# Swapping high and low weight products in every second column block of a two-layer trunk

## The chip, the cores and the metric

The kernel runs on one core of a Trainium2 chip. The metric is the device time of one launch in microseconds. The kernel before took 800.97 us (median of three runs, 798.78 to 801.15). All rows below are from one profiled execution, which took 801.64 us; its instructions span 799.9 us.

## The reference

Two pre-norm residual layers on 256 tokens of width 1024, in float32. Cut to what matters:

```
h = x
for i in range(2):
    hn = rmsnorm(h, norm_mix[i])
    h = h + (short_conv_mixer(hn) if i == 0 else dilated_attention_mixer(hn))
    h = h + square(relu(rmsnorm(h, norm_mlp[i]) @ mlp_w_up[i])) @ mlp_w_down[i]
    h = h + sigmoid(rmsnorm(h, norm_ple[i]) @ ple_w_gate[i]) * (p[i] @ ple_w_proj[i])
return rmsnorm(h, norm_final)
```

Layer 0's mixer is a gated short convolution (`h @ w_in` split into B, C and X, then `w_out`). Layer 1's is attention with 8 heads in 3 groups, with rotary on part of each head. Nearly all of the arithmetic is the product of 256 token rows with large weight matrices: about 140 MB of weights are read once.

## The kernel before

**Split products.** A float32 product is built from products of rounded parts. Each weight slab arrives by DMA as `raw` (128 partitions by up to 1024 columns, 512 KB). ScalarE (ACT) rounds it to `whi` (L332, in `split_to`), and VectorE (DVE) makes the rest `wlo = raw - whi` (L281, in `sub`). Activations are split the same way into a pair tile, high part and low part side by side. A product then needs high by high, high by low and low by high.

**Three kinds of block.** `block` (L364 issues every weight matmul) has three forms, named by the plan. Kind "n" issues three matmuls of 256 columns into one half of an accumulator. Kind "t" swaps the operands, with 384 or 512 columns. Kind "w", the one that the change touches, issues two: a short one of 256 columns (`wlo` against the high activations) and a long one of 512 columns (`whi` against high and low activations side by side), into an accumulator (one PSUM bank) of its own. Each matmul has its own 128 by 128 weight load, shown as PEld.

**The plan.** `make_plan` writes out by hand the order of all blocks. In kind "w" two neighbouring column blocks, half 0 and half 1, always follow each other for the same row block `k`, each into its own bank: half 0, half 1, next `k`, half 0, half 1. Kind "w" is used in the X part of the convolution's input (accumulators `acc_X`), in both MLPs' up products (`acc_u`), in three quarters of the down products (`acc_d`; the last quarter is kind "n"), and in the query and key products of heads 1 to 7 (`acc_qk`). Behind the last row block stands a step that adds the two halves of each accumulator, one copy on ACT (L383) and one add on DVE (L384) for half 0 and then for half 1.

**The order on the engines.** TensorE (PE) takes the blocks in the plan's order. For ACT, DVE and GpSimd (POOL) a scheduler decides, from modelled times, how the steps' instructions and the weight splits are interleaved. Each engine takes its own queue in order. There are five `raw` and six split buffers, so splits run up to five slabs ahead of PE.

**Attention's side work.** For each head and group the added sums go to POOL, which applies the rotary (L607, L610, L616, the step `qk_out`). For group 0 the result is split again on ACT (L403) and DVE (L281, `qk<-qk,qk`). The step `scores` (PE L639, L642) writes two banks, DVE takes the masked maximum (L645, L648), ACT the exponential (L649) and the scaling (L651), and the step `turn` transposes the result on PE (L660, `tp`).

Of the kernel before, what the change touches and what calls it, by code (L numbers as in the profile page):

```python
# [205 lines left out]
def width(key):  # L206
    return {"v": GROUPS, "gate1": 4, "proj1": 4}.get(key, 1)
# [32 lines left out]
def tile_trunk(ctx: ExitStack, tc: tile.TileContext, plan, slabs, ap, out):  # L240
# [25 lines left out]
    def bank(name):  # L266
        return psum.tile([P, 2, S], F32, tag="ps", name=name)
# [9 lines left out]
    def flat(t):  # L277
        return t.rearrange("p i s -> p (i s)")
# [57 lines left out]
    def weights(item):  # L336
        si, at = place[item]
        split_to(si + min(LOOK, 1 + si // 3))
        hi, lo = parts[si]
        n = width(item[0]) * P  # L340
        return hi[:, at : at + n], lo[:, at : at + n]

    def block(kind, key, k, col, name, half, operand, m=0, cuts=1):
        name = (*name, half) if kind == "w" else name
        if name not in opened:
            acc[name] = bank("acc_" + "_".join(map(str, name)))
        left[name, half if kind == "n" else 0] -= 1
        whi, wlo = weights((key, k, col))
        x = state[operand][k // 2]
        if kind == "n":  # L350
            dst = acc[name][:, half, :]
            products = ((dst, wlo, x[0][:, k % 2, :]), (dst, whi, x[1][:, k % 2, :]), (dst, whi, x[0][:, k % 2, :]))
        elif kind == "w":

            dst = acc[name]
            products = ((dst[:, 0, :], wlo, x[0][:, k % 2, :]), (flat(dst), whi, flat(x[2][:, k % 2, :, :])))
        else:
            n = width(key) * P // cuts
            whi, wlo = (t[:, m * n : (m + 1) * n] for t in (whi, wlo))
            dst = flat(acc[name])[:, :n]  # L360
            xhi, xlo = (t[:, k % 2, half * P : (half + 1) * P] for t in x[:2])
            products = ((dst, xhi, whi), (dst, xhi, wlo), (dst, xlo, whi))
        for n, (to, a, b) in enumerate(products):
            nc.tensor.matmul(  # L364
                to,
                a,
                b,
                start=n == 0 and name not in opened,
                stop=n == len(products) - 1 and left[name, half if kind == "n" else 0] == 0,
                skip_group_check=True,  # L370
            )
            opened.add(name)
# [394 lines left out]
    for op in plan:  # L767
        if op[0] != "do":
            block(*op)
        elif op[1] in URGENT:  # L770
            with tc.high_priority(offset=HURRY):
                steps[op[1]](*op[2:])
        else:
            steps[op[1]](*op[2:])
# [87 lines left out]
```

## Time and profile before

| What | us |
|---|---|
| Median of three runs | 800.97 |
| Profiled execution | 801.64 |
| Span of its instructions | 799.9 |
| PE busy | 780.3 (98%) |
| DVE busy | 583.1 (73%) |
| ACT busy | 442.6 (55%) |
| POOL busy | 179.0 (22%) |

The profile's page lists busy time by engine, the granted TensorE clock in 40 slices, the chain that ended last, and groups of instructions by source line. A matmul's end is modelled, so the duration of one says less than the distance between the starts of two. In the groups, `lo` and `hi` in a tile's name are the low and high part of the weights.

### The profile page before, as it was taken

How to read it: one execution, taken by the hardware profiler on the slowest of the kernel's cores; microseconds unless marked ns; L12 is line 12 of the kernel's file. 1: busy time of each engine (PE TensorE's matmuls, PEld its weight loads, DVE VectorE, ACT ScalarE, POOL GpSimd, SP SyncE). 2: the span in 40 equal slices, each digit the busy share in tenths (PEclk: the TensorE clock that was granted, in tenths of full speed). 3: DMA queues.
4: the chain of work that ended last, by engine and by line, in shares of the span. 5: the costliest groups of instructions: out<-in, count | busy, mean ns of one | idle time of the engine just before them, and what ended most of it. 6: DMA issues, size and time to landing. Idle time of an engine off the chain costs nothing.

```text
span 799.9 us, 12768 instructions
## 1 busy us (share of the span) xinstructions
PE 780.3 (98%) x4986; PEld 713.9 (89%) x4986; DVE 583.1 (73%) x818; ACT 442.6 (55%) x672; POOL 179.0 (22%) x117
## 2 busy tenths in 40 slices
PE   8999999999999999995999999999999999999996
PEld 8999998888888999985999999999988888888985
DVE  6987778898456669747688779778598777555555
ACT  7655565666444447526647546656475655444453
POOL 0000000000000000397487678668000000000001
PEclk9999999999999999998999999999999999999998
DMA  8865565555555555643464455447556656556521
GB/s 280 298 213 192 182 187 176 193 180 189 184 184 186 185 165 170 197 125 103 161 185 157 150 168 169 158 148 213 172 155 185 196 183 188 183 185 186 184 79 54
DMA packets 41676, 140.98 MB, mean 176 GB/s; under 512 B 4752, under 2 KB 5136, under 8 KB 41616
## 3 DMA queue, kind: packets, MB, share of 16 engines
q1 hardware_dynamic: 41616, 140.17, 55.3%
q8 instruction: 39, 0.64, 0.3%
q14 instruction: 21, 0.17, 0.1%
HBM read 139.10 MB, written 1.05 MB: 175 GB/s over the span
## 4 chain that ended last, share of the span: by engine, by line
PE 89%; POOL 3%; DVE 3%; ACT 1%; issue 1%; DMA 1%; SPq 0%; POOLq 0%; DVEq 0%; ACTq 0%
PE acc_d L364 23%; PE acc_u L364 23%; PE acc_qk L364 13%; PE acc_v L364 7%; PE acc_o L364 6%; PE acc_g L364 5%; PE acc_B L364 3%; PE acc_X L364 3%; PE acc_C L364 3%; POOL rot L610 2%; DVE wlo L281 1%; PE tp L660 1%; PE o L681 1%; PE sc L642 1%; POOL qk L616 1%
## 5 line engine op out<-in xcount | busy, mean ns | idle before, releaser
L281 DVE TENSOR_TENSOR wlo<-raw,whi 128x1024 fp32r<-128x1024 f32 (+3 forms) x273 | 366.8, 1353 | 130.2 <-ACT whi L332 129.2
L332 ACT ACTIVATE whi<-raw 128x1024 fp32r<-128x1024 f32 (+3 forms) x273 | 276.4, 1017 | 191.3 <-PE acc_d L364 88.3
L364 PE MATMUL acc_d<-u,whi 128*128 128x512 f32 (+1 forms) x640 | 181.8, 352 | 0.0
L364 PE MATMUL acc_u<-x,whi 128*128 128x512 f32 x512 | 181.0, 399 | 0.0
L364 PE MATMUL acc_d<-u,wlo 128*128 128x256 f32 x512 | 144.1, 281 | 0.0
L364 PE MATMUL acc_u<-x,wlo 128*128 128x256 f32 x512 | 143.7, 281 | 0.0
L364 PE MATMUL acc_qk<-x,whi 128*128 128x512 f32 (+1 forms) x432 | 134.5, 368 | 0.0
L364 PEld LDWEIGHTS acc_d<-u,whi 128*128 128x128 f32 x640 | 112.1, 190 | 18.1
L436 POOL TENSOR_TENSOR n<-v,power 128x4 f32<-128x4 f32 (+1 forms) x6 | 6.5, 1085 | 516.7 <-DVE v L456 514.0
L364 PEld LDWEIGHTS acc_u<-x,whi 128*128 128x128 f32 x512 | 96.1, 188 | 23.8
L364 PE MATMUL acc_qk<-x,wlo 128*128 128x256 f32 x384 | 107.8, 281 | 0.0
L364 PEld LDWEIGHTS acc_d<-u,wlo 128*128 128x128 f32 x512 | 97.1, 190 | 0.0
L364 PEld LDWEIGHTS acc_u<-x,wlo 128*128 128x128 f32 x512 | 96.7, 189 | 0.0
L364 PEld LDWEIGHTS acc_qk<-x,whi 128*128 128x128 f32 x432 | 77.8, 188 | 13.6
L610 POOL TENSOR_TENSOR rot<-qk,sinr 16x512 f32<-16x512 f32 x48 | 88.2, 1838 | 3.3
L364 PEld LDWEIGHTS acc_qk<-x,wlo 128*128 128x128 f32 x384 | 72.4, 189 | 0.0
L364 PE MATMUL acc_v<-whi,x 128*128 128x384 f32 x256 | 69.4, 342 | 0.0
L607 POOL TENSOR_TENSOR qk<-qk,cosr 128x512 f32<-128x512 f32 x24 | 37.6, 1565 | 56.2 <-DVE qk L384 39.5
L364 PEld LDWEIGHTS acc_v<-whi,x 128*128 128x128 f32 x256 | 47.0, 190 | 0.0
L364 PE MATMUL acc_o<-y,whi 128*128 128x256 f32 x256 | 46.0, 283 | 0.0
L616 POOL TENSOR_TENSOR qk<-qk,rot 48x512 f32<-48x512 f32 x24 | 43.7, 1822 | 1.7
L364 PE MATMUL acc_v<-wlo,x 128*128 128x384 f32 x128 | 43.1, 337 | 0.0
(164 smaller groups left out, 1036.4 us busy)
## 6 DMA issues: line engine op xcount, KB each, us to landing
raw<-in_w SPq DMA_DIRECT2D x232, 512.0 KB, 3.6
raw<-in_w SPq DMA_DIRECT2D x32, 384.0 KB, 3.1
raw<-in_w SPq DMA_DIRECT2D x7, 256.0 KB, 5.3
h<-in_xT SPq DMA_DIRECT2D x4, 256.0 KB, 5.6
out<-ht SPq DMA_DIRECT2D x4, 256.0 KB, 2.0
pt<-in_pT SPq DMA_DIRECT2D x2, 256.0 KB, 4.4
mask<-in_mask SPq DMA_DIRECT2D x2, 256.0 KB, 4.2
gain<-in_gain SPq DMA_DIRECT2D x2, 256.0 KB, 4.3
```

What stands on the lines that cost most here:

```text
L281: nc.vector.tensor_tensor(out, a, f32(b), ALU.subtract)
L332: nc.scalar.activation(hi[:, :width], t[:, :width], AF.Copy)
L364: nc.tensor.matmul(to, a, b, start=n == 0 and name not in opened, stop=n == len(products) - 1 and left[name, half if kind == "n" else 0] == 0,
L436: nc.gpsimd.tensor_tensor(y, v, power[:, : v.shape[1]], ALU.pow)
L607: nc.gpsimd.tensor_tensor(t, p, both(cosr), ALU.mult)
L610: nc.gpsimd.tensor_tensor(r[dst : dst + 16], p[src : src + 16], sinr[src : src + 16].unsqueeze(1).to_broadcast([16, 2, S]), ALU.mult,)
L616: nc.gpsimd.tensor_tensor(t[:48], t[:48], r[:48], ALU.add)
L642: nc.tensor.matmul(ps[:, (g + 1) * P : (g + 2) * P], t[:, 0, own], t[:, 1, own], start=True, stop=True)
L660: nc.tensor.transpose(ps[n // 2][:, n % 2, b * P : (b + 1) * P], sm[:, n * P : (n + 1) * P], ident)
L681: nc.tensor.matmul(ps[:, 0, b * P : (b + 1) * P], v12[:, b, g * P : (g + 1) * P], t[:, g, b * P : (b + 1) * P], start=False, stop=g == 1, ...
```

## The change

Where the block is the second of two neighbours (`half` is 1) and of kind "w", its two matmuls change places: the long one with `whi` comes first and the short one with `wlo` behind it. The first of the two keeps its order. Two lines stand more in the source, so every line below them has a number that is higher by two (L364 becomes L366).

```
@@ -354,6 +354,8 @@
 
             dst = acc[name]
             products = ((dst[:, 0, :], wlo, x[0][:, k % 2, :]), (flat(dst), whi, flat(x[2][:, k % 2, :, :])))
+
+            products = products[::-1] if half else products
         else:
```

On PE, in the X part of the convolution, before (the digit behind `acc_X_0` is the half; 128x256 is the short one):

```order
67 L364 MATMUL acc_X_0_0_335<-x0_0_139,whi9_274 128x512
68 L364 MATMUL acc_X_0_1_350<-x0_0_139,wlo9_275 128x256
69 L364 MATMUL acc_X_0_1_350<-x0_0_139,whi9_274 128x512
70 L364 MATMUL acc_X_0_0_335<-x0_0_139,wlo9_275 128x256
71 L364 MATMUL acc_X_0_0_335<-x0_0_139,whi9_274 128x512
```

The same place after the change:

```order
67 L366 MATMUL acc_X_0_0_335<-x0_0_139,whi9_274 128x512
68 L366 MATMUL acc_X_0_1_350<-x0_0_139,whi9_274 128x512
69 L366 MATMUL acc_X_0_1_350<-x0_0_139,wlo9_275 128x256
70 L366 MATMUL acc_X_0_0_335<-x0_0_139,wlo9_275 128x256
71 L366 MATMUL acc_X_0_0_335<-x0_0_139,whi9_274 128x512
```

Short, long, short, long has become short, long, long, short. This happens at 648 pairs of blocks; PE's order is otherwise the same, except that at the first `acc_u` of layer 1 before had short, short, long, long.

The scheduler answers on ACT and DVE. On ACT, where the sums of head 4, group 0 are made, before:

```order
344 L332 ACTIVATE whi157_4727<-raw157_4625 128x768
345 L383 ACTIVATE qk_4_0_4747<-acc_qk_4_0_0_4701 128x256
346 L383 ACTIVATE qk_4_0_4747<-acc_qk_4_0_1_4710 128x256
347 L332 ACTIVATE whi158_4792<-raw158_4643 128x768
348 L649 ACTIVATE sm3_0_4765,st2_3_0_4768<-sm3_0_4765,st1_3_0_4767 128x512
```

The same place after the change:

```order
344 L332 ACTIVATE whi157_4727<-raw157_4625 128x768
345 L385 ACTIVATE qk_4_0_4747<-acc_qk_4_0_0_4701 128x256
346 L332 ACTIVATE whi158_4792<-raw158_4643 128x768
347 L385 ACTIVATE qk_4_0_4747<-acc_qk_4_0_1_4710 128x256
348 L651 ACTIVATE sm3_0_4765,st2_3_0_4768<-sm3_0_4765,st1_3_0_4767 128x512
```

A weight split now stands between the copies of half 0 and half 1. The same happens at nearly every sum of two halves, on ACT and on DVE (there `wlo158` moves in front of the add of half 1).

On DVE, where the scores of head 0 are taken (`sc0`, with the sums of head 1 around them), before:

```order
358 L384 TENSOR_TENSOR qk_1_2_3964<-acc_qk_1_2_0_3888,qk_1_2_3964 128x256
359 L384 TENSOR_TENSOR qk_1_2_3964<-acc_qk_1_2_1_3897,qk_1_2_3964 128x256
360 L645 ISA sm0_0_3940,st0_0_0_3941<-sc0_0_3934,mask0_3461 128x512
361 L645 ISA st0_0_0_3941 128x1
362 L281 TENSOR_TENSOR wlo132_3977<-raw132_3834,whi132_3976 128x1024
363 L648 TENSOR_SCALAR st1_0_0_3942<-st0_0_0_3941 128x1
364 L645 ISA sm0_1_3955,st0_0_1_3956<-sc0_1_3949,mask1_3463 128x512
365 L645 ISA st0_0_1_3956 128x1
366 L648 TENSOR_SCALAR st1_0_1_3957<-st0_0_1_3956 128x1
```

The same place after the change:

```order
358 L386 TENSOR_TENSOR qk_1_2_3964<-acc_qk_1_2_0_3888,qk_1_2_3964 128x256
359 L647 ISA sm0_0_3940,st0_0_0_3941<-sc0_0_3934,mask0_3461 128x512
360 L647 ISA st0_0_0_3941 128x1
361 L386 TENSOR_TENSOR qk_1_2_3964<-acc_qk_1_2_1_3897,qk_1_2_3964 128x256
362 L650 TENSOR_SCALAR st1_0_0_3942<-st0_0_0_3941 128x1
363 L647 ISA sm0_1_3955,st0_0_1_3956<-sc0_1_3949,mask1_3463 128x512
364 L647 ISA st0_0_1_3956 128x1
365 L281 TENSOR_TENSOR wlo132_3977<-raw132_3834,whi132_3976 128x1024
366 L650 TENSOR_SCALAR st1_0_1_3957<-st0_0_1_3956 128x1
```

The split `wlo132` has moved from behind the first maximum to behind the second; the same nine instructions stand in front of and including `st1_0_1`. POOL's and SP's orders are unchanged.

## Rows read from the trace of the kernel before

**Rows 1.** The page: busy us (share) and instructions; the chain by engine.

```profile
PE 780.3 (98%) x4986; PEld 713.9 (89%) x4986; DVE 583.1 (73%) x818; ACT 442.6 (55%) x672; POOL 179.0 (22%) x117
PE 89%; POOL 3%; DVE 3%; ACT 1%; issue 1%; DMA 1%; SPq 0%; POOLq 0%; DVEq 0%; ACTq 0%
```

**Rows 2.** PE's waits: engine, line, waited for; us in total, times, longest.

```profile
PE tp L660 <- ACT sm L651: 8.7, 1, 8.7
```

**Rows 3.** The chain in order of time: start us, us, engine, tile, line, matmuls.

```profile
48.96 5.76 PE acc_C L364 x48
54.72 5.64 PE acc_X L364 x32
...
530.76 11.11 PE acc_qk L364 x64
...
603.62 67.84 PE acc_u L364 x384
671.46 90.87 PE acc_d L364 x576
762.33 5.47 PE acc_g L364 x24
```

**Rows 4.** Groups by line and shape: how many long matmuls of kind "w".

```profile
L364 PE MATMUL acc_u<-x,whi 128*128 128x512 f32 x512 | 181.0, 399 | 0.0
L364 PE MATMUL acc_d<-u,whi 128*128 128x512 f32 x384 | 135.8, 399 | 0.0
L364 PE MATMUL acc_qk<-x,whi 128*128 128x512 f32 x336 | 117.2, 392 | 0.0
L364 PE MATMUL acc_X<-x,whi 128*128 128x512 f32 x64 | 22.8, 398 | 0.0
```

**Rows 5.** Timeline of PE and PEld in an up product: start us, us.

```profile
160.45 0.28 PE L364 MATMUL acc_u<-x,wlo 128*128 128x256 f32 x1
160.45 0.19 PEld L364 LDWEIGHTS acc_u<-x,whi 128*128 128x128 f32 x1
...
160.57 0.40 PE L364 MATMUL acc_u<-x,whi 128*128 128x512 f32 x1
...
160.81 0.28 PE L364 MATMUL acc_u<-x,wlo 128*128 128x256 f32 x1
```

**Rows 6.** Timeline of PE at the first `acc_u` of layer 1.

```profile
580.54 0.40 PE L364 MATMUL acc_u<-x,wlo 128*128 128x256 f32 x2
580.78 0.70 PE L364 MATMUL acc_u<-x,whi 128*128 128x512 f32 x2
581.31 0.28 PE L364 MATMUL acc_u<-x,wlo 128*128 128x256 f32 x1
```

**Rows 7.** Timeline of PEld there.

```profile
580.74 0.30 PEld L364 LDWEIGHTS acc_u<-x,whi 128*128 128x128 f32 x2
```

**Rows 8.** Timeline of DVE, then ACT, around the scores of head 0.

```profile
367.24 2.32 DVE L281 TENSOR_TENSOR wlo<-raw,whi 128x1024 fp32r<-128x1024 f32 x1
...
370.26 0.15 DVE L648 TENSOR_SCALAR st<-st 128x1 f32<-128x1 f32 x1
...
370.45 0.72 ACT L649 ACTIVATE sm<-sm,st 128x512 f32<-128x512 f32 x1
```

**Rows 9.** Timeline of ACT, DVE and POOL in head 4; then PE's chain.

```profile
442.21 0.84 ACT L332 ACTIVATE whi<-raw 128x768 fp32r<-128x768 f32 x1
...
451.43 0.71 ACT L651 ACTIVATE sm<-sm,st 128x512 f32<-128x512 f32 x1
...
440.09 1.71 DVE L281 TENSOR_TENSOR wlo<-raw,whi 128x768 fp32r<-128x768 f32 x1 [0.26 <-ACT whi L332]
...
453.44 6.40 DVE L281 TENSOR_TENSOR wlo<-raw,whi 128x768 fp32r<-128x768 f32 x3 [0.25 <-ACT whi L332]
...
442.85 1.28 POOL L607 TENSOR_TENSOR qk<-qk,cosr 128x512 f32<-128x512 f32 x1 [1.87 <-DVE qk L384]
...
454.61 0.87 PE tp L660 x8
```

More of the change, by code (lines that the diff above doesn't have):

```diff
@@ L356, in block @@
             products = ((dst[:, 0, :], wlo, x[0][:, k % 2, :]), (flat(dst), whi, flat(x[2][:, k % 2, :, :])))
+            products = products[::-1] if half else products
         else:
```

## The prediction

> **What bounds the kernel now.** The page comes first. PE is busy for 780.3 us of the span of 799.9, and the chain that ended last is PE for 89% of it [rows 1]. So the end moves only if PE's own work gets shorter or longer, or if PE waits at a place where it doesn't now. PE's waits come second: the one of any size is 8.7 us, once, where the transposes of head 0 wait for ACT's scaled scores [rows 2]. The chain in order of time comes third, because it gives the price of a matmul by division, which the single durations don't (their ends are modelled and overlap).
>
> From the chain [rows 3], short and short: 5.76 us / 48 = 120 ns for a 256-column matmul behind its like. Long and long: 5.47 / 24 = 228 ns for a 512-column one behind its like. So a matmul costs (228 - 120) / 256 = 0.42 ns a column and some 12 ns on top, and a pair of short and long should cost 348 ns. The query and key pairs of the heads cost just that: 11.11 / 32 = 347 ns. The other pairs of the same form do not: X 5.64 / 16 = 352.5 ns, up 67.84 / 192 = 353.3 ns, and down, with its last quarter of 192 short matmuls taken off, (90.87 - 192 x 0.120) / 192 = 353.3 ns. These pairs pay 6.3 ns more than a head's pair does, and the reader is to see that no column, load or wait in the rows accounts for it.
>
> The timeline of an up product says where it is paid [rows 5]: the short one starts at 160.45, the long at 160.57, the next short at 160.81. Short to long is 0.12 us, as among equals; long to short is 0.24 where 0.228 would do. The weight load of the next matmul starts when the present one starts and takes 0.19, so loads run beside the matmuls in this order too.
>
> **The change, part by part.**
>
> *PE's order.* No matmul, load, column or wait is added or removed. Two pairs, short-long-short-long, become short-long-long-short. Per two pairs there were two steps from short to long and two from long to short; now there is one of each, one long-long and one short-short. Affected are the long matmuls of kind "w": 64 in X, 512 up, 384 down, together 960 that pay 6.3 ns, and 336 in the heads that pay nothing extra [rows 4].
>
> What the new steps cost: long-long 228 and short-short 120, from the rows above. What becomes of the 6.3 ns, no row of a whole stage shows, since there the order alternates always. The bounds: if each step from long to short goes on paying its extra, half of those steps remain and 960 x 6.3 / 2 = 3.0 us go. If the extra belongs to strict alternation, all of it goes, 6.1 us. If it belongs to a short and a long together, whatever their order, nothing goes.
>
> One place of before holds the new order by accident, the first up product of layer 1 [rows 6]: two short from 580.54, two long from 580.78, the next short at 581.31. These four take 0.77 us, but the first of the two high loads starts at 580.74 [rows 7], where it would have started with the second short at 580.66, that is 0.08 late. Without that the four take 0.69 us, against 2 x 353.3 = 707 ns for two pairs of up and 694 for two of the heads. Read to 0.01 us, it is nearer to the price without the extra, but it is one place right behind a stall. I take the middle between half and all, 4.6 us, and keep 3.0 and 6.1 as ends of this case. In the heads I take nothing, for 228 + 120 is what their pairs cost.
>
> *ACT's and DVE's order.* The scheduler now puts a weight split between the sums of half 0 and half 1. In the MLPs and in X nobody waits for these sums soon: the banks come round after several column blocks, and the activations are used by the next product many slabs later. That cover is the reason for a price of nothing; PE has no row there that waits [rows 2].
>
> In the heads the sum of group 0 starts a chain: POOL's rotary starts at 442.85 in head 4 as soon as DVE has added half 1, ACT waits for POOL, and behind that ACT scales the scores of the head before, until 451.43 + 0.71 = 452.14; PE takes their transposes at 454.61 [rows 9]. So the chain has 2.47 us to spare. The split in front adds its ACT part, 0.84 us, and its DVE part, 1.71 us for a split of this size as DVE takes it in the row nearest by. The two overlap nothing in the worst case: 2.55 us, 0.1 us over in each of five heads. But the sum of half 0 on DVE runs beside ACT's split, and in before the split stood in front of the score chain as well (wlo158 behind the first maximum), which it no longer does. I take nothing. The upper bound uses a split beside a busy POOL, 6.40 / 3 = 2.13 us: 0.84 + 2.13 - 2.47 = 0.5 us in five heads, 2.5 us.
>
> At the one wait of 8.7 us, what ends last is ACT's scaling for head 0. It stands behind the exponential of the second bank at 370.45, which follows DVE's second negated maximum at 370.26 [rows 8]. In front of that maximum the same DVE instructions stand before and after, the split of 2.32 us among them; only their order differs. So the wait ends where it ended: price 0, between -0.5 us (a small instruction that now comes earlier) and +1.0 us (half a split, if DVE has to wait for ACT, whose copy of half 1 now stands behind a split).
>
> *What PE does not keep.* Gains in layer 0 carry through: everything behind them starts earlier, the POOL chain in front of the 8.7 us too.
>
> **Sum.** 801.64 us for the profiled execution less 4.6 is 797.0. The profiled execution is 0.67 us above the median of the runs, 800.97, so against the median the forecast is 796.4 us.
>
> **A page that speaks against it.** The rows give 120 ns for 256 columns and 228 for 512, each in a run of its like. The Trainium skill, in "TensorE: Matmul & The Clock Gate", section "Back-to-back issue gap", gives the gap of a matmul from its own columns alone, columns / 2.4 plus 2.5 ns, so that an order could not matter; by that a pair would be 325 ns and the change worth 0. The rows disagree with the size, 347 and 353 ns, and the difference between stages of one form shows that something beside the columns counts.
>
> **The rivals.**
>
> *Order does not count.* The extra goes with the stage and not with the neighbours: same matmuls, same 353.3 ns a pair, 801.0 us. For it: the extra is as constant in X as in up and down, with other tiles in each; and the heads, with the same order, don't pay it, so order alone can't be its cause. The gap formula of "TensorE: Matmul & The Clock Gate" in the Trainium skill, named above, would have it so too. Against it: it is paid at one kind of step, long to short [rows 5], and the one place in the new order reads lower [rows 6, 7].
>
> *The score chain comes too late.* In heads 3 to 7 the split in front of the second sum pushes the rotary, the scaled scores and then the transposes past 454.61. It decides from a delay of 2.47 us on; at its upper bound it costs 2.5 us, and if the cadence gives nothing back the time is 803.5 us, slower than before. For it: PE has no other work to put there, and POOL and DVE share this stretch. Against it: the bound needs every split at its slowest.
>
> *Long behind long costs more than 228 ns.* The two long matmuls of rows 6 and the short behind them are 0.53 us apart, 0.074 over 0.456. I put that down to the late load. If it were the price of two high loads in a row, 648 places would cost 48 us, 849 us. Against it: other long matmuls follow each other at 228 ns [rows 3].
>
> That the change doesn't do what it says is out: the order shows the swap at 648 places.
>
> **How the numbers follow.** The forecast, a gain between 3.0 and 6.1 us in the cadence, has a chance of 0.57; order does not count, 0.26; the late score chain with no gain, or a small loss of another kind, 0.13; dear long pairs, 0.04. The likeliest case's own range is 794.4 to 798.5 (the ends of the cadence with 0.5 us each way). The range for 8 in 10 reaches over the second case and most of the third: 793.8 to 803.0. A measurement here tells about 0.3%, 2.4 us, from no change. Of the forecast case, a twentieth falls within that by runs' scatter, and some of the order-free case falls on either side: faster 0.57, same 0.27, slower 0.16.
>
> **What will show it.** Right: the chain's up stretch of 192 pairs shorter than 67.84 us, near 66.9 (all of the extra gone would be 66.6, half 67.2); X below 5.64 for 32 matmuls; the heads' 64 matmuls still 11.1; PE's wait for `sm` still about 8.7; in the heads no new PE wait on ACT. Wrong: 353 ns a pair as before, or a PE wait at `tp` in heads 3 to 7, or long matmuls more than 228 ns behind long ones.

## The result, and the profile after

| | before | after |
|---|---|---|
| Median, same series | 801.15 us (5 runs) | 796.24 us (5 runs) |
| Lowest to highest | 798.78 to 801.31 | 795.37 to 797.34 |
| Profiled execution / span | 801.64 / 799.9 | 797.34 / 795.5 |

The ratio after to before is 0.9937, with a 95% interval of 0.9924 to 0.995: 4.9 us faster. The forecast was 796.4 us. As the sections below show, the total comes out right partly by luck, because terms that the prediction set at nothing offset each other, and the cause behind its one term was seen too simply.

The page of the changed kernel, busy time by engine, to lay beside [rows 1]:

```profile
PE 776.2 (98%) x4986; PEld 711.6 (89%) x4986; DVE 582.1 (73%) x818; ACT 436.6 (55%) x672; POOL 177.2 (22%) x117
```

PE's busy time fell by 4.1 us, about as much as the span. PE does the same matmuls in less time; it is not mainly waiting less.

The chain in order of time, changed kernel (start us, us, what), beside [rows 3]:

```profile
38.62 5.58 PE acc_X L366 x32
...
286.52 5.76 PE acc_g L366 x48
...
368.81 1.97 PE tp L662 x8
...
373.94 5.58 PE acc_qk L366 x32
...
528.50 11.17 PE acc_qk L366 x64
...
578.48 22.50 PE acc_u L366 x128
601.21 66.89 PE acc_u L366 x384
668.10 89.92 PE acc_d L366 x576
758.02 5.47 PE acc_g L366 x24
```

Five rows of the same view of the kernel before, to measure stretches against:

```profile
37.55 5.65 PE acc_X L364 x32
...
287.88 5.76 PE acc_g L364 x48
...
371.93 1.97 PE tp L660 x8
376.58 5.55 PE acc_qk L364 x32
...
580.70 22.68 PE acc_u L364 x128
```

A pair of up now takes 66.89 / 192 = 348.4 ns (353.3 before), one of X 5.58 / 16 = 348.8 (352.5), and one of down (89.92 - 192 x 0.120) / 192 = 348.3 (353.3). A pair in the heads takes 11.17 / 32 = 349 where it took 347: the cheap pairs became dearer. Gates did not change (5.76 for 48, 5.47 for 24).

The starts give a balance. From X at 37.55 to the gate at 287.88 before took 250.33 us, now 247.90: -2.43. From the gate to `tp` it was 84.05 and is 82.29: -1.76, nearly all of it PE's wait there. From `tp` to the heads' first pairs it is 5.13 instead of 4.65: +0.48. The heads to layer 1's first up product take 204.54 instead of 204.12: +0.42. From there to the next gate it is 179.54 instead of 181.63: -2.09. The start, up to 37.55, became 1.07 longer; that is scatter of one execution, as the other profiles of the new order reach the same place at 36.8 to 37.1. In all: -4.3, against -4.4 in the span, whose last piece is within 0.1.

PE's waits in the changed kernel (us in total, times, longest), beside [rows 2]:

```profile
PE tp L662 <- ACT sm L653: 7.0, 1, 7.0
PE acc_p L366 <- DVE wlo L281: 2.2, 3, 1.4
```

The wait for head 0 is 1.7 us shorter than [rows 2] has it. The second row is the start's scatter. No transposes of heads 3 to 7 wait.

### The profile page after: what moved, and what is told of

Read it like the earlier page. It is cut to its first block, busy times and chain, and to the rows that moved or that the text cites. A ratio compares the mean times of both kernels' runs of the same rounds, so it can differ in the third digit from the quotient of the medians.

```text
span 795.5 us, 12797 instructions
## 1 busy us (share of the span) xinstructions
PE 776.2 (98%) x4986; PEld 711.6 (89%) x4986; DVE 582.1 (73%) x818; ACT 436.6 (55%) x672; POOL 177.2 (22%) x117
## 4 chain that ended last, share of the span: by engine, by line
PE 87%; DVE 5%; POOL 3%; ACT 2%; issue 2%; DMA 1%; SPq 0%; POOLq 0%; DVEq 0%; ACTq 0%
PE acc_d L366 23%; PE acc_u L366 22%; PE acc_qk L366 13%; PE acc_v L366 7%; PE acc_o L366 6%; PE acc_g L366 5%; PE acc_B L366 2%; PE acc_X L366 2%; DVE wlo L281 2%; PE acc_C L366 2%; POOL rot L612 2%; PE tp L662 1%; PE o L683 1%; PE sc L644 1%; ACT whi L332 1%
## 5 line engine op out<-in xcount | busy, mean ns | idle before, releaser
L366 PE MATMUL acc_d<-u,whi 128*128 128x512 f32 (+1 forms) x640 | 166.8, 351 | 0.0
L366 PE MATMUL acc_u<-x,whi 128*128 128x512 f32 x512 | 161.0, 396 | 0.0
L366 PE MATMUL acc_qk<-x,whi 128*128 128x512 f32 (+1 forms) x432 | 122.9, 371 | 0.0
L366 PEld LDWEIGHTS acc_u<-x,wlo 128*128 128x128 f32 x512 | 96.4, 188 | 22.4
L366 PEld LDWEIGHTS acc_d<-u,wlo 128*128 128x128 f32 x512 | 96.9, 189 | 17.0
L366 PE MATMUL acc_d<-u,wlo 128*128 128x256 f32 x512 | 111.8, 279 | 0.0
L366 PE MATMUL acc_u<-x,wlo 128*128 128x256 f32 x512 | 101.3, 278 | 0.0
L366 PEld LDWEIGHTS acc_d<-u,whi 128*128 128x128 f32 x640 | 98.5, 190 | 0.0
L366 PEld LDWEIGHTS acc_qk<-x,wlo 128*128 128x128 f32 x384 | 72.4, 188 | 14.2
L366 PE MATMUL acc_qk<-x,wlo 128*128 128x256 f32 x384 | 82.5, 281 | 0.0
L366 PEld LDWEIGHTS acc_u<-x,whi 128*128 128x128 f32 x512 | 78.0, 189 | 0.1
L366 PE MATMUL acc_v<-whi,x 128*128 128x384 f32 x256 | 69.8, 343 | 0.0
L366 PEld LDWEIGHTS acc_qk<-x,whi 128*128 128x128 f32 x432 | 66.1, 189 | 0.0
L366 PEld LDWEIGHTS acc_v<-whi,x 128*128 128x128 f32 x256 | 47.4, 191 | 0.0
L366 PE MATMUL acc_o<-y,whi 128*128 128x256 f32 x256 | 46.0, 284 | 0.0
L366 PE MATMUL acc_v<-wlo,x 128*128 128x384 f32 x128 | 43.3, 339 | 0.0
```

The costliest lines, as they stand in the source:

```text
L366: nc.tensor.matmul(to, a, b, start=n == 0 and name not in opened, stop=n == len(products) - 1 and left[name, half if kind == "n" else 0] == 0,
```

## Experiments

All but numbers 5, 6 and 8, which have one execution each, were timed against the kernel before in their own series, whose medians were 801.97 (the first four), 802.16 (the next four) and 801.41 (the last two). Ratios stand with their 95% intervals. "Slow" and "fast" below mean a cadence of 353.3 and of 346.7 ns a pair of short and long.

### 1. The new order everywhere but in the heads

```
-            products = products[::-1] if half else products
+            products = products[::-1] if half and key != "qkv" else products
```

> Swap in X, up and down, but not in the heads' query and key pairs. Neighbour theory (the gain is the alternation of short and long broken up, stage by stage): X, up and down cost 348.4 ns a pair as in the changed kernel (384 up matmuls in 66.9 us), the heads go back to 347 ns (64 matmuls in 11.10 us instead of 11.17); 336 pairs x 2 ns = 0.7 us less than the changed kernel, 795.6 us. Scheduler theory (the gain comes from the order on ACT and DVE): the 8.7 us wait of head 0, shorter by 1.7 us in the changed kernel, goes back and the time is 798.

Measured: 797.15 us (796.56 to 798.78), ratio 0.9954 (0.994 to 0.9968). Chain rows of this kernel:

```profile
127.92 66.89 PE acc_u L366 x384
...
382.93 11.10 PE acc_qk L366 x64
```

X, up and down alone carry most of the gain. The heads went back to 347 ns a pair and the wait at `tp` to 8.7 us. Both expectations held in part and both missed the time: the neighbour theory named the pairs, the scheduler theory the wait, and 796.2 - 0.7 + 1.7 = 797.2 us is what was measured.

### 2. The new order in the heads alone

```
+            products = products[::-1] if half and key == "qkv" else products
```

> Swap only in the heads' query and key pairs. Neighbour theory: X, up and down cost 353.3 ns a pair as before (384 up matmuls in 67.84 us), the heads 349 ns; 0.7 us more than before on PE, less what the wait of head 0 gives (1.7 us if ACT's and DVE's order around head 1 is what shortened it): 800 to 802 us, no difference that can be told. Scheduler theory: most of the gain is there, 797 to 798 us.

Measured: 800.60 us (798.41 to 802.11), ratio 0.9995 (0.9977 to 1.0013). That is what the neighbour theory expected. Up stayed at 67.84, the heads took 11.16 to 11.17 for 64, and the wait at `tp` was 6.9. With experiment 1 this separates the parts: the cadence gain belongs to X, up and down, the 2 ns lost a pair and the 1.7 us of shorter wait to the heads.

It also held something that neither theory had. Layer 1's first up stretch, in the old order, ran at 346.7 ns behind a late start:

```profile
580.21 22.27 PE acc_u L366 x128
602.71 67.84 PE acc_u L366 x384
```

22.27 for 64 pairs, with a late load of 0.08 us at the start like that of [rows 6], is the fast cadence (22.19 / 64 = 346.7), 67.84 for 192 the slow one. Same stage, tiles and form; between them stand two statistics matmuls of 256 columns (`ssq`).

### 3. Strict alternation again, but the long one first

```
+            products = products[::-1]
```

> Both halves take the long product first: long, short, long, short. The alternation is back, with the high part first everywhere. Neighbour theory: 353.3 ns a pair in X, up and down, 347 in the heads, 801 us as before. Rival (the high part is ready earlier than the low one, so taking it first helps): at least the changed kernel's gain, 796 us or less.

Measured: 798.37 us (797.10 to 801.09), ratio 0.9974 (0.9957 to 0.9991). The theory of neighbours named 801 and fell, because the two cadences changed places within layer 1. The chain:

```profile
128.82 67.84 PE acc_u L366 x384
...
579.10 22.85 PE acc_u L366 x128
602.19 66.56 PE acc_u L366 x384
668.75 89.59 PE acc_d L366 x576
```

In layer 0 up runs slow. In layer 1 it starts slow (22.85 holds some 0.24 us of a late start), and from the same two `ssq` matmuls on it is fast, 66.56 / 192 = 346.7, through down's three quarters of kind "w" as well. PE's timeline at the switch (start us, us):

```profile
601.78 0.41 PE L471 MATMUL ssq<-sums,ones_r 128*128 128x256 f32 x2
```

The rival fell too: the long one comes first everywhere, and layer 0 is as slow as before. So another theory was needed: a strict alternation has two cadences, holds whichever it has, and may change it where something breaks in.

### 4. The other half swapped

```
+            products = products if half else products[::-1]
```

> The first half is swapped and the second is not: long, short, short, long. Round the loop the same chain of neighbours as in the changed kernel, shifted by two. Neighbour theory: 348.4 ns a pair, 796 us. Rival (which accumulator's short matmul comes last matters, by the order that the scheduler makes of the sums): between 796 and 801 us, with 348.4 ns a pair but a longer wait elsewhere.

Measured: 797.98 us (797.38 to 800.14), ratio 0.9965 (0.9947 to 0.9984); up 66.88, heads 11.16 for 64, wait at `tp` 8.7. For the cadence it does not matter which half is swapped. For the wait it does, as the rival had it: it is shorter only where half 1 takes the long one first.

### 5. Foreign matmuls in the old order

Single matmuls of 128 to 512 columns, whose sums nobody reads, were put in front of six column pairs of each up product, to break into the alternation.

```
+TICKS = {5: 256, 7: 384, 9: 128, 11: 320, 13: 512, 14: 256}
+        if j in TICKS:
+            plan.append(("do", "tick", x, TICKS[j]))
```

> The order of before, with one extra matmul into a spare bank in front of the up product's column pairs 5, 7, 9, 11, 13 and 14 in both layers, of 256, 384, 128, 320, 512 and 256 columns (the extra sums are not used). Mode theory (the alternation runs in one of two cadences, 353.3 or 346.7 ns a pair, and what breaks into the run decides which, for as long as the run lasts): some stretches between extra matmuls go at 346.7 and some at 353.3, nothing between for long, and the down product keeps the cadence of the last stretch. Stage theory (up and down cost 353.3 by what they read and write, heads 347): every stretch stays at 353.3 in both layers.

Measured: 801.97 us (one execution). The chain, in layer 0:

```profile
145.49 11.29 PE acc_u L367 x64
156.85 11.15 PE acc_u L367 x64
...
179.68 5.54 PE acc_u L367 x32
185.34 11.31 PE acc_u L367 x64
```

11.29 / 32 = 353 ns and 5.54 / 16 = 346: one stage shows both, changing at foreign matmuls and nowhere else. The row of 11.15 is fast too: its first step, behind the foreign matmul of 128 columns, came 0.05 us late, and (11.15 - 0.05) / 32 = 347. Down behind the last stretch was slow, as that was (90.88). Which sizes flip it was not a rule: those of 128 and 512 columns gave the fast cadence in layer 0 and the slow one in layer 1, that of 384 the reverse.

### 6. The same foreign matmuls in the new order

```
             products = products[::-1] if half else products
+TICKS = {5: 256, 7: 384, 9: 128, 11: 320, 13: 512, 14: 256}
```

> The changed kernel with the same extra matmuls. Mode theory in its strong form (short, long, long, short has one cadence, whatever it starts from): 348.3 to 348.4 ns a pair in every stretch of both layers, X, heads and down too. If the new order has modes too, some stretch differs from 348.4 by more than 1 ns.

Measured: 797.44 us (one execution). Layer 0, two of the stretches, and PE's timeline where the first of them starts:

```profile
156.43 11.20 PE acc_u L369 x64
...
184.85 11.16 PE acc_u L369 x64
```

```profile
156.26 0.33 PE L369 MATMUL acc_u<-x,wlo 128*128 128x256 f32 x1
156.43 0.39 PE L369 MATMUL acc_u<-x,whi 128*128 128x512 f32 x1
```

By the rows 348 to 350 ns, and 351.6 in layer 1's first stretch (22.50 for 64 pairs), which is more than the expectation's 1 ns. The excess is at the starts: here the first short one takes 0.17 us to the long one instead of 0.12, in layer 1 the first steps are 0.2 late. Between the starts of matmuls, from the ninth of each stretch on, it is 347.6 to 349.1 ns in every stretch of X, up and down. Short-long-long-short has one cadence.

### 7. Four short, then four long

If each change of length had a price, fewer changes would be cheaper still. The blocks of kind "w" were gathered by four: four short matmuls, then the four long ones.

```
+        if kind == "w":
+            four.append((key, k, col, name, half, operand))
+            if len(four) == 4:
+                for part in (0, 1):
+                    for item in four:
+                        single(part, *item)
+                four.clear()
+            return
```

> Four blocks at a time (two row blocks by two halves): four short ones, then four long ones. Theory that each step from long to short costs extra: one such step in four pairs, so less than the changed kernel's 348.4, down to 347.3 ns, 795.5 us. Mode theory (the slow cadence needs the alternation, and what is left over the own prices is nothing): 348 to 348.4 ns, 796 to 797 us. In either, 353.3 nowhere.

Measured: 800.98 us (799.64 to 802.97), ratio 0.9988 (0.9978 to 0.9999). Both expectations missed. Its up product:

```profile
128.44 67.36 PE acc_u L353 x384
```

67.36 / 192 = 350.8 ns, dearer than the new order; and the wait at `tp` was 8.7 us. So "fewer changes of length" is no rule, and the best order cannot be derived from the prices of single steps.

### 8. The kernel before, profiled again

> The kernel before, a second profile. Mode theory: X, up and down at 353.3 and heads at 346.7 again if what they start from is the same in every execution; another mix of just these two cadences if it isn't. Stage theory: the same prices at the same stages.

Measured: 800.78 us (one execution). The chain at the start of layer 1:

```profile
580.24 22.27 PE acc_u L364 x128
```

Its timeline there, beside [rows 6]:

```profile
580.32 0.71 PE L364 MATMUL acc_u<-x,whi 128*128 128x512 f32 x2
580.86 0.28 PE L364 MATMUL acc_u<-x,wlo 128*128 128x256 f32 x1
```

The first profile of the same kernel had 22.68 here, 64 slow pairs behind a late load [rows 6]; this one has 64 fast pairs behind the same late load (the two long ones take 0.54 us to the next short one, 0.08 more than 0.46). From the ninth matmul on the starts of this stretch give 353.2 ns a pair in the first profile and 346.7 in this one. The rest was as before. The cadence is not fixed by the stage: the same instructions take either, by execution.

### 9. The heads long-first in both halves

```
-            products = products[::-1] if half else products
+            products = products[::-1] if half or key == "qkv" else products
```

> Short-long-long-short stays in X, up and down, and in the heads both halves take the long matmul first (long, short, long, short). Theory, two cadences for a strict alternation and one for short-long-long-short, with the head-0 wait set by half 1's order in the heads: X, up and down as in after (up 66.9 for 384), the wait at tp 7.0, and the heads in the fast cadence, 346.7 ns a pair (11.1 us for 64): 336 x 2.3 ns = 0.8 us less than after, about 795.5 us where after is 796.2. Rival one, the heads' alternation falls into the slow cadence behind the scores: 353.3 ns a pair, 11.3 us for 64, 336 x 4.3 ns = 1.4 us more than after, 797.7. Rival two, the short wait belongs to short-long-long-short in the heads and not to half 1's long one coming first: wait 8.7, about 797.2.

Measured: 795.97 us (794.29 to 797.12), ratio 0.9931 (0.9912 to 0.9951). The chain:

```profile
366.98 1.97 PE tp L662 x8
368.95 3.84 PE acc_v L366 x12
372.79 5.70 PE acc_qk L366 x32
...
381.70 11.10 PE acc_qk L366 x64
```

The heads are in the fast cadence, 11.10 for 64, and the wait at `tp` is 7.0, as the theory says. Only the first 32 matmuls behind the wait (5.70) are in the slow one, 353.0 ns a pair between starts, so rival one held at this one place. Each later head takes 29.06 us against 29.16 in experiment 10. Five such heads make 0.5 us. They don't show in the time, which experiment 10 gives.

### 10. The changed kernel again, beside experiment 9

> The changed kernel once more, to compare the other one of this call with, and to see whether its cadence varies by execution as that of the kernel before did. Theory (one cadence for short-long-long-short): 348.3 to 349 ns a pair in every stage again, layer 1's first up stretch included, up 66.9 for 384; 796.2 us. Rival (it has two as well, and one profile showed one of them by chance): some stretch of 384 at 66.6 or at 67.8.

Measured: 795.84 us (795.34 to 797.37), ratio 0.9936 (0.9919 to 0.9953). The same stretch, and layer 1's first up stretch:

```profile
369.05 3.47 PE acc_v L366 x12
372.53 5.57 PE acc_qk L366 x32
...
381.31 11.16 PE acc_qk L366 x64
...
577.10 22.52 PE acc_u L366 x128
```

PE's timeline at the start of layer 1:

```profile
576.93 0.28 PE L366 MATMUL acc_u<-x,wlo 128*128 128x256 f32 x1
...
577.73 0.40 PE L366 MATMUL acc_u<-x,wlo 128*128 128x256 f32 x2
```

Every stage showed 348 to 349 ns a pair again. Layer 1's first up stretch is one of them: its first three steps take 0.80 us instead of 0.58, and (22.52 - 0.22) / 64 = 348.4. So the single cadence is not the chance of one profile. Experiment 9 has no lead: behind the wait its v blocks and first query pairs take 3.84 + 5.70 us, here 3.47 + 5.57, which eats 0.5 (some 0.07 of it the slow cadence of those 32). The granted clock there, in the window from 370 to 373 us (start:end, length, busy time by engine, clock, DMA share, GB/s), first of experiment 9, then of 10:

```profile
370.00:373.00 3.00, 3.00 (x11) 2.96 (x11) 3.00 (x3) 1.89 (x5) 2.94 (x2) 0.54 0.45 131
```

```profile
370.00:373.00 3.00, 3.00 (x14) 2.91 (x13) 3.00 (x3) 2.25 (x6) 2.94 (x2) 0.67 0.40 131
```

In the 3 us ahead of it the granted clock is 0.50 in both, the lower of the two levels (1.2 of 2.4 GHz), and in the 3 us behind it 1.00; in this window experiment 9 has it back later, 0.54 against 0.67 on average. From `tp` to the first query pairs it took between 4.65 us (before) and 5.81 (experiment 9), so the 0.5 is within what this recovery varies: behind the same 8.7 us of wait it took 4.65 us in the kernel before and 5.81 in experiment 7.

## Why the prediction was right, and where it was not

**PE's order, 4.6 us of gain.** Right in size. The measured pairs give 64 x 3.7 + 512 x 4.9 + 384 x 5.0 ns = 4.7 us; the balance has 2.43 + 2.09 = 4.5, without X's first stretch. The middle between "half" and "all" was a choice between readings of a mechanism that is neither, so that it came out is in part luck. Where the old order pays was read rightly: between starts, long to short is 236.5 ns on average in up and 230 to 232 in the fast heads, while short to long is 115 to 117 in both. But this step has no price of its own. Strict alternation can have either of two cadences, and the new order has a third one between them, in which long to short is 233.4. Where before would have been in the fast cadence throughout, the change would have cost 960 x 1.7 ns = 1.6 us in X, up and down instead of winning.

**The page weighed against it.** By the formula of the Trainium skill, "TensorE: Matmul & The Clock Gate", section "Back-to-back issue gap", a pair would take an estimated 325 ns in any order. The section gives it for a single matmul by itself, and says that in a stream of weight loads and matmuls both set the spacing, about 131 ns at 512 columns. No row bears out either figure: long behind long is 228 ns [rows 3], and 346.7, 348.4, 350.8 and 353.3 a pair for one and the same set of matmuls show that the order counts.

**Heads, 0.** Mis-sized: "228 + 120 is what their pairs cost" priced single steps, and experiment 7 shows that these don't add up. The pairs were in the fast cadence and went to 349: 0.42 us lost in the balance, undone in experiment 1.

**The wait at head 0, 8.7 us unchanged, between -0.5 and +1.0.** This step failed: 7.0, a gain of 1.7 us outside its bounds. The count was right, nine DVE instructions up to the second maximum in both; the step erred in taking each at a fixed duration, though the prediction's own bound for heads 3 to 7 had a split at 1.71 us and beside a busy POOL at 2.13 [rows 9]. Rows of the kernel before, DVE's and POOL's timeline, to go with [rows 8]:

```profile
361.60 0.69 DVE L281 TENSOR_TENSOR qk<-qk,qk 128x512 fp32r<-128x512 f32 x1 [8.48 <-ACT qk L403]
...
363.03 1.93 POOL L607 TENSOR_TENSOR qk<-qk,cosr 128x512 f32<-128x512 f32 x1 [2.13 <-DVE qk L384]
363.82 2.23 DVE L281 TENSOR_TENSOR wlo<-raw,whi 128x1024 fp32r<-128x1024 f32 x1
...
367.22 1.25 POOL L610 TENSOR_TENSOR rot<-qk,sinr 16x512 f32<-16x512 f32 x1
```

And of the changed kernel:

```profile
360.23 0.69 DVE L281 TENSOR_TENSOR qk<-qk,qk 128x512 fp32r<-128x512 f32 x1 [8.47 <-ACT qk L405]
...
362.45 1.23 DVE L281 TENSOR_TENSOR wlo<-raw,whi 128x1024 fp32r<-128x1024 f32 x1
362.67 2.13 POOL L609 TENSOR_TENSOR qk<-qk,cosr 128x512 f32<-128x512 f32 x1 [3.14 <-DVE qk L386]
...
364.88 1.26 POOL L612 TENSOR_TENSOR rot<-qk,sinr 16x512 f32<-16x512 f32 x1
365.53 1.69 DVE L281 TENSOR_TENSOR wlo<-raw,whi 128x1024 fp32r<-128x1024 f32 x1
367.15 0.14 DVE L650 TENSOR_SCALAR st<-st 128x1 f32<-128x1 f32 x1
```

Two splits of 1024 columns stand in this chain. Before, the first starts 0.79 us behind a POOL instruction and takes 2.23, the second takes 2.32 [rows 8]. Now the first starts 0.22 ahead of POOL's and takes 1.23, while POOL's takes 2.13; the second takes 1.69. Together that is 4.55 against 2.92, 1.63 of the 1.7 us. From DVE's first instruction here to the second maximum it was 8.66 (361.60 to 370.26) and is 6.92. What a split takes beyond 1.23 us is what is left of POOL's instruction when it starts, less 0.14: 1.00 of 1.14 left and 1.09 of 1.23 before, 0.46 of 0.61 now. So it is in all 77 splits of 1024 columns that start during a POOL tensor instruction in these two profiles, and the 372 that meet none take 1.20 to 1.23 us. The Trainium skill, "SBUF — State Buffer", section "Who interferes with whom", says that a DVE instruction with two inputs in SBUF contends with a GpSimd one that reads SBUF, and that the order of issue decides which of the two blocks. The rows agree (1.23 ahead, 2.23 behind). That half 1's order in the heads decides the wait is shown: 6.9 to 7.0 with the long one first there (experiments 2, 3, 6, 9, 10), 8.7 without (1, 4, 5, 7, 8). In all twelve profiles the two splits take 2.22 to 2.23 and 2.32 us with the long wait, 1.23 and 1.68 to 1.69 with the short one. That it works through POOL is read from these rows; no run changed that alone.

**Gain from the wait, loss behind it.** The prediction let the stall's end carry through. In this profile 0.48 us of the 1.7 was lost between `tp` and the heads, the stretch of the low clock; as experiment 10 shows, that stretch varies by more than this between executions, so the loss can't be put down to the change.

**MLP and X, ACT and DVE reordered, 0; score chain of heads 3 to 7, 0.** Right: no such wait of PE appeared. The split in front of half 1 costs nothing there.

**The rivals.** "Order does not count" fell with experiments 1 and 10. Its remark that something beside the order must matter, because the heads did not pay, was right. "Long behind long costs more" fell: in the new order long to long is 232.8 ns, the mean distance of such starts in up and down, 5 above 228, but short to short is 114.6, 5 below 120. The late score chain did not come.

**Sum.** 4.52 in the cadence and 1.76 in the wait, less 0.42 in the heads, 0.48 behind the wait and 1.07 of scatter at the start, is 4.3 us. The forecast had 4.6 from one term alone. What there is to gain depends on the cadences that the kernel before takes in an execution: in the four series 13 of its 64 were below 800 us, and layer 1's up and down in the fast cadence would be 448 x 6.6 ns = 3.0 us. No such execution of it was profiled, so that this is the reason is not shown.

## What to carry to other kernels

Price a mixed stream of matmuls by the period of a whole pattern in a profile, in every stage and in more than one execution: single steps did not add up here. Where strict alternation of two sizes shows two periods, an order with a single one between them may win what the slow one costs, and loses a little where the fast one ruled. When DVE and GpSimd work side by side, which of them starts first sets a duration, so a reordering with the same instructions can still move a wait.

## What the hardware showed beyond that

- Matmuls of 256 and 512 columns in strict alternation had two cadences. Between starts, from the ninth matmul of a stretch on, every stretch ran at 346.6 to 346.7 or at 353.0 to 354.1 ns a pair (140 stretches in seven profiles), none between. The same instructions took either, by execution (experiment 8), and it held through whole stages, 133 us of up and down in layer 1 of experiment 3. Changes within a product came at other matmuls in it (experiments 2, 3 and 5).
- It is no even chance: without foreign matmuls layer 0 was slow in every profile of this order, the heads fast in all stretches but one (experiment 9).
- Short-long-long-short ran at 347.5 to 349.1 in every stretch whatever came before (the changed kernel, experiments 1, 2, 6, 9 and 10), and four and four at 350.8 in up (experiment 7).
- A DVE split beside POOL takes longer by what is left of POOL's instruction, less 0.14 us; the one that starts first is not slowed.
- What in the chip makes the two cadences stays open. Stretches of one product, with the same tiles and the same engines beside them, showed both in experiment 5, so these alone don't set it; no run here went further.
